# An attention stage in which half of the probabilities' turns move from TensorE to VectorE and a trip through DRAM

## The chip, the cores and the metric

The kernel runs on one core of one Trainium2 chip. The metric is device time in microseconds, from the start to the end of one execution; lower is better. The engines are named as in the profile: PE is TensorE (matmuls and transposes), DVE is VectorE, ACT is ScalarE, POOL is GpSimd, SP is SyncE, which here only issues DMAs. Profiles come from one profiled execution.

## The reference

One layer of a diffusion backbone over 1024 latent tokens and 256 context tokens, model width 1024, in float32: a SwiGLU feed-forward half step, then a short convolution branch beside an attention branch, merged by gates, then a second feed-forward half step. The part that matters here is the attention: 8 query heads and 2 key/value heads of 128, each latent query reads all 256 context keys and all 1024 latent keys in one softmax.

```python
def gqa_attend(q, k, v):
    s = jnp.einsum('btkgd,blkd->bkgtl', q, k, preferred_element_type=jnp.float32) * (HEAD_DIM ** -0.5)
    p = jax.nn.softmax(s, axis=-1).astype(v.dtype)
    return jnp.einsum('bkgtl,blkd->btkgd', p, v)
...
        k_all = jnp.concatenate([k_c, k_l], axis=1)
        v_all = jnp.concatenate([v_c, v_l], axis=1)
        o_l = latent_attention(q_l, k_all, v_all)

        x = x + ml[5] * merge_branches(y_conv_l, o_l, gt_l, w_branch_conv[layer],
                                       w_branch_attn[layer], w_out[layer])
```

## The kernel before

A product of two float32 matrices is made of three TensorE passes: each operand is split into a high part (a cast to the format float32r, on ScalarE) and a low part (the operand less its high part, on VectorE or GpSimd), and `mm3` adds high x high, high x low and low x high in one PSUM bank. `split` makes both parts.

The stages follow one another: token norms and the first feed-forward product, its output product, the mixing projections (convolution, gates, queries, keys, values), attention with the convolution branch's output product as filler, the merge of both branches, the second feed-forward step, the final norm. Nearly all tiles of 128 x 1024 float32 (4 KB a partition) come from one pool, `apool`, with 38 buffers under one tag. Weights pass through `wpool` (tags `raw`, `wh`, `wl`), short-lived 128 x 512 tiles through `tpool`. PSUM has five banks under tag `s`, two under `t` and one under `o`. The framework orders the instructions of each engine from the order of the program and a simulated timeline; where `strict` is set or an instruction is pinned, program order stays. Every engine and DMA queue works in its order.

Attention is made of 16 units (`Unit`): 8 heads by two halves of 512 queries. For a unit:
- `begin` splits the 512 queries.
- `scores(qt)`, for each of four tiles of 128 queries: TensorE makes the scores against 256 context keys and twice 512 latent keys; VectorE takes the maxima (`m3`) and the negative maximum (`nm`); ScalarE writes the exponentials to `pc` (context) and `pl` (latent, one tile of 128 x 1024 for each `qt`) with their sums (`rs`), which VectorE adds to `rsum`.
- `turn(kt)`, for each of ten key tiles (two of context, eight latent): queries stand on the partitions of `pc` and `pl`, but the product with the values needs the keys there. TensorE transposes four blocks of 128 x 128 into a PSUM bank `pt`; `split` writes the high and low parts `pts`.
- `values(kt)`: three passes with the parts of the values, added over the ten key tiles in the bank `po`.
- `inverse`: VectorE takes the reciprocals of the sums, GpSimd stores them to DRAM (`rinvd`) and loads them back as a row for all partitions (`rrow`). `output`: ScalarE copies `po` over the queries' place, GpSimd multiplies by the row.

The loop over the units runs one behind itself. While unit n makes its scores, `seconds` turns the ten key tiles of unit n - 1, three of them ahead of their `values` (`AHEAD`), and `fillers` gives single steps of the convolution branch's output product (`conv_out`, whose weights are brought in by `conv_weights` two outputs ahead). After each of the four `scores`, 3, 2, 3 and 2 steps of `seconds` are taken. The fillers are used up before the last units. After the last unit its remaining turns are mixed with `merge`, the product with the attention branch's weights. In the last units `split_output` makes the parts of finished heads on GpSimd.

Of the kernel before, what the change touches and what calls it, by code (L numbers as in the profile page):

```python
# [18 lines left out]
P = 128  # L19
D = 1024  # L20
KD = D // P
# [16 lines left out]
A_BUFS = 38  # L38
# [13 lines left out]
def tile_dit_layer(  # L52
# [52 lines left out]
    dram = ctx.enter_context(tc.tile_pool(name="dram", bufs=1, space=DRAM))  # L105

# [6 lines left out]
    def atile(name, shape=(P, SLOT), dt=F32):  # L113
        return apool.tile(list(shape), dt, tag="A", name=uniq(name))

# [333 lines left out]
    class Latents:  # L449


        def __init__(self, name):
            self.name, self.t = name, {}

        def pair(self, k, i):
            if (k, i) not in self.t:
                self.t[k, i] = atile(self.name, (P, 2, 512))
            return self.t[k, i]
# [6 lines left out]
    class Context:  # L465
        def __init__(self, name, dt=F32):
            self.t = [atile(name, (P, 4, CT), dt) for _ in range(2)]
# [49 lines left out]
    def fetch_rows(w, js):  # L517

        ts = {j: atile("raw") for j in js}
        for j, t in ts.items():  # L520
            load(t[:], w[j * P : (j + 1) * P, :])
        return ts
# [11 lines left out]
    class Winograd:  # L534
# [6 lines left out]
        def __init__(self, xs, gain, mod, m, pairs, plain=False, ahead=3, side_from=None):  # L541
# [12 lines left out]
            self.source, self.ready = self.lefts(pairs, side_from), []  # L554

        def keep(self, i, k, src, lo_eng=None):

            t = atile(f"r{i}", (P, 2, 512), F32R)
# [40 lines left out]
        def norm1(self, turned=None):  # L599
# [8 lines left out]
            def scaled(k):  # L608
                t22[k] = ttile("h22")
                if self.plain:  # L610
                    self.r[0][k] = atile("h12", (P, 2, 512))
                    t12[k] = self.r[0][k][:, 0]
# [26 lines left out]
        def part_second(self, k):  # L639

            t = self.r[0][k]
            h = atile("r0", (P, 2, 512), F32R)
            split(t[:, 0], h[:, 0], h[:, 1])
# [133 lines left out]
        def start_by_half(self):  # L777

            uc = [atile("uc", (P, 2, 512)) for _ in range(2)]
# [23 lines left out]
            for j in range(BY_HALF, self.n_ahead):  # L803
                t = atile("uc", (P, 2, 512))
# [39 lines left out]
    class Rows:  # L844


        def __init__(self, src, n, name):
# [3 lines left out]
            for k, m in self.groups:  # L851
                for lower in range(2):
                    if m == 1:
                        t = atile(name, (P, 2, 512))
# [21 lines left out]
    def row_products(w, rows, add, after=lambda i, k: None, halves=False):  # L876
# [12 lines left out]
        s1, s2, w11 = {}, {}, {}  # L889
# [13 lines left out]
        def parts(src, where):  # L903
# [3 lines left out]
            else:  # L907
                if where == "kept":
                    t = atile("kept", (P, 2, 512), F32R)
# [19 lines left out]
        def second_sum(k, m):  # L929
            s2[k] = atile("ws", (P, 2, 512))[:, :m]  # L930
# [3 lines left out]
        def sums(i, g):  # L934
# [11 lines left out]
            if i == 1 and g >= 3 or i == 4 and g < n - 3:  # L946
                k, m = groups[g - 3 if i == 1 else n - 3 + g]
                s1[k] = atile("ws", (P, 2, 512))[:, :m]
# [94 lines left out]
    xs, xc = Latents("x"), Context("xc")  # L1043

    def fetch_tokens(ch):
# [3 lines left out]
        for j in range(n // P):  # L1049
            t = atile("xtok")  # L1050
# [168 lines left out]
    def side(j, bank=ps_o):  # L1219
        pc = bank()  # L1220

        def do(i, w):
# [9 lines left out]
            if i == 4:  # L1232
                if j % 2 == 0:
                    hid_c[j // 2] = atile("hidc", (P, 4, CT), F32R)
# [45 lines left out]
    for j in range(NH):  # L1280
# [6 lines left out]
        if j == SIDE_FROM - 1:  # L1287
# [10 lines left out]
            for token in range(2):  # L1298
                c_acc.append(atile("cacc"))
# [31 lines left out]
    xs = Latents("x1")  # L1331
# [67 lines left out]
    for i in range(KD):  # L1399
        u = atile("u")  # L1400
# [47 lines left out]
    rope_t = [atile("rope", (P, KD, HD)) for _ in range(2)]  # L1448
    for i in range(2):
        sp.dma_start(out=rope_t[i][:], in_=rope[i])  # L1450
    hg = atile("hg", (P, 2, HD))
# [171 lines left out]
    class Unit:  # L1623
# [3 lines left out]
        def begin(self):  # L1627
            self.qs = [ttile("qs", dt=F32R) for _ in range(2)]
            split(q_of(self.hd, self.ch), *self.qs)
            self.pc = atile("pc", (P, 4, CT))  # L1630
            self.pl = []
            self.rsum = small("rsum", 4)

        def scores(self, qt):
# [9 lines left out]
            if self.hd == 0 and self.ch[1] == 0 and qt < 2:  # L1644
                pl = wpool.tile([P, SLOT], F32, tag="raw", name=uniq("pl"), bufs=3)
            else:
                pl = atile("pl")
            self.pl.append(pl)
            for j in range(2):
# [4 lines left out]
                parts.append((pl[:, j * 512 : (j + 1) * 512], ps))  # L1654
# [3 lines left out]
            dve.reduce_sum(out=self.rsum[:, qt : qt + 1], in_=rs[:], axis=AX.X)  # L1658

        def turn(self, kt):  # L1660
# [18 lines left out]
        def inverse(self):  # L1679
# [3 lines left out]
            pool.dma_start(out=row.rearrange("(j p) -> p j", p=P), in_=rinv[:])  # L1683
            self.rows = ttile("rrow")
            pool.dma_start(out=self.rows, in_=row.partition_broadcast(P))
# [270 lines left out]
```

## Time and profile before

| | |
|---|---|
| median of 3 runs | 2629.52 us (2629.28 to 2633.78) |
| profiled execution | 2628.72 us |
| its span, first to last instruction | 2626.9 us |
| busy: PE, DVE, ACT, POOL | 2604.6, 1988.4, 1167.3, 546.3 us |
| mean granted TensorE clock | 0.998 |
| DMA | 384.71 MB, mean 146 GB/s |

How to read it: busy time is the time in which an engine had an instruction in work; on TensorE matmuls are pipelined and their durations overlap, so a price of one is read from start to start. A row of instructions names line, engine, operation, the tile written and the tiles read, then the count; in grouped rows there follow busy time, mean duration in ns, and the idle time of the engine before them with what ended it. All instructions stand under line 90, the helper that records them, so groups are told apart by the names of tiles.

### The profile page before, as it was taken

To read this page: it belongs to the slowest core of one execution; us is meant where nothing else is said; L and a number is where in the kernel's file an instruction comes from. 1 tells how busy PE (TensorE), PEld (TensorE's weight loads), DVE (VectorE), ACT (ScalarE), POOL (GpSimd) and SP (SyncE) were. 2 spreads that over 40 slices of the span, in tenths; PEclk is the share of its full clock that TensorE was granted. 3 is DMA by queue.
4 is the path that set the end of the run, shared out by engine and by line. 5 is a ranking of instruction groups with operands and counts; after the bars stand their busy time and mean duration, and the time that the engine had idled before them with its cause. 6 is when DMAs were issued, how large, how long until landed. Compare 5 with 4: busy or idle time off the path is not lost.

```text
span 2626.9 us, 35317 instructions
## 1 busy us (share of the span) xinstructions
PE 2604.6 (99%) x12643; PEld 2173.7 (83%) x12643; DVE 1988.4 (76%) x3339; ACT 1167.3 (44%) x2322; POOL 546.3 (21%) x425
## 2 busy tenths in 40 slices
PE   8999999999999999999999999999999999999998
PEld 5888898888888888888888888888888888888888
DVE  5889866878897888977788666675457786667996
ACT  6533454333454642333345566574237223334553
POOL 0135201221010034333022112132000442321100
PEclk9999999999999999999999999999999999999999
DMA  9666475335973364532522322114525653227831
GB/s 325 205 205 200 138 216 172 119 118 201 311 185 117 127 204 158 171 126 90 200 76 92 79 87 65 33 37 121 160 81 177 196 172 97 89 84 279 197 82 65
DMA packets 377321, 384.71 MB, mean 146 GB/s; under 512 B 24102, under 2 KB 260792, under 8 KB 377144
## 3 DMA queue, kind: packets, MB, share of 16 engines
q1 hardware_dynamic: 367704, 363.53, 42.7%
q0 software_dynamic: 9440, 18.91, 4.2%
q8 instruction: 99, 1.62, 0.3%
q14 instruction: 78, 0.64, 0.1%
HBM read 310.45 MB, written 71.86 MB: 146 GB/s over the span
## 4 chain that ended last, share of the span: by engine, by line
PE 93%; DVE 3%; DMA 1%; ACT 1%; SPq 1%; issue 0%; DVEq 0%; ACTq 0%
PE ps L90 80%; PE pt L90 7%; PE po L90 6%; DMA rawm<-in_w_mod_dram 1%; SPq L90 1%; DVE xb L90 0%; DVE wl L90 0%; DVE m L90 0%; DVE macc L90 0%; ACT x L90 0%; DVE pts L90 0%; DVE nt L90 0%; ACT r L90 0%; DMA half<-in_ffn_w_in_dram 0%; DVE y L90 0%
## 5 line engine op out<-in xcount | busy, mean ns | idle before, releaser
L90 PE MATMUL ps<-r,wl 128*128 128x512 f32 x5196 | 1197.1, 390 | 2.6 <-ACT r L90 1.6
L90 PEld LDWEIGHTS ps<-r,wl 128*128 128x128 f32 x5196 | 972.5, 188 | 205.5 <-ACT r L90 1.8
L90 ACT CAST wl<-sum 128x512 fp32r<-128x512 f32 x218 | 133.8, 621 | 317.7 <-PE ps L90 240.7
L90 ACT CAST wl<-raw 128x512 fp32r<-128x512 f32 x287 | 177.7, 620 | 206.5 <-PE ps L90 155.6
L90 DVE TENSOR_TENSOR wl<-raw,wl 128x512 fp32r<-128x512 f32 x287 | 208.9, 731 | 63.3 <-ACT wl L90 61.8
L90 POOL TENSOR_TENSOR sum<-raw 128x512 f32<-128x512 f32 x55 | 79.6, 1447 | 688.0 <-DMA raw<-in_w_in_dram 221.7
L90 DVE TENSOR_TENSOR wl<-sum,wl 128x512 fp32r<-128x512 f32 x218 | 191.4, 879 | 37.6 <-ACT wl L90 36.4
L90 DVE TENSOR_TENSOR u<-u,ps 128x512 f32<-128x512 f32 x186 | 126.5, 680 | 33.1 <-PE ps L90 33.0
L90 DVE SCALAR_TENSOR_TENSOR macc<-rawm,silu_r,macc 128x512 f32<-128x512 f32 x165 | 136.7, 850 | 17.0 <-DMA rawm<-in_w_mod_dram 16.8
L90 ACT CAST rh<-hid 128x512 fp32r<-128x512 f32 x132 | 81.7, 621 | 135.5 <-PE ps L90 109.6
L90 DVE TENSOR_TENSOR pts<-pt,pts 128x512 fp32r<-128x512 f32 x160 | 107.2, 685 | 36.1 <-ACT pts L90 34.3
L90 POOL TENSOR_TENSOR sum<-raw,sum 128x512 f32<-128x512 f32 x55 | 76.7, 1394 | 273.0 <-DVE wl L90 270.0
L90 DVE TENSOR_REDUCE m<-ps 128x1 f32<-128x256 f32 (+1 forms) x192 | 110.9, 596 | 29.5 <-PE ps L90 28.4
L90 ACT CAST pts<-pt 128x512 fp32r<-128x512 f32 x160 | 92.2, 597 | 85.5 <-PE pt L90 84.6
L90 PE MATMUL ps<-rh,wl 128*128 128x512 f32 x360 | 122.1, 390 | 0.0
L90 PE MATMUL ps<-wh,r 128*128 128x512 f32 x384 | 120.4, 393 | 0.0
L90 ACT CAST wh<-raw 128x512 fp32r<-128x512 f32 (+1 forms) x85 | 68.1, 802 | 108.4 <-PE ps L90 86.2
L90 DVE TENSOR_TENSOR rl<-hid,rh 128x512 fp32r<-128x512 f32 x132 | 90.1, 686 | 27.9 <-ACT rh L90 15.8
L90 PE MATMUL ps<-kl,qs 128*128 128x512 f32 x384 | 104.0, 394 | 0.1
L90 PE MATMUL ps<-rh,wh 128*128 128x512 f32 x300 | 102.2, 389 | 0.0
L90 PE MATMUL ps<-y,wc 128*128 128x512 f32 x384 | 95.3, 391 | 0.2 <-DVE g L90 0.2
L90 POOL TENSOR_TENSOR sum<-sum,raw 128x512 f32<-128x512 f32 x55 | 88.0, 1601 | 6.0 <-PE ps L90 4.0
(333 smaller groups left out, 5064.9 us busy)
## 6 DMA issues: line engine op xcount, KB each, us to landing
raw<-in_ffn_w_in_dram SPq DMA_DIRECT2D x131, 512.0 KB
raw<-in_ffn_w_out_dram SPq DMA_DIRECT2D x72, 512.0 KB
rawm<-in_w_mod_dram SPq DMA_DIRECT2D x136, 256.0 KB
raw<-in_w_in_dram SPq DMA_DIRECT2D x64, 512.0 KB
hid<-hd SPq DMA_DIRECT2D x40, 512.0 KB
ucd<-uc SPq DMA_DIRECT2D x33, 512.0 KB
ws<-in_ffn_w_out_dram POOLq DMA_DIRECT2D x26, 512.0 KB, 6.1
hd<-c SPq DMA_DIRECT2D x42, 256.0 KB
```

The lines of the kernel that those rows point to most:

```text
L90: inst = getattr(self.engine, name)(*args, **kw)
```

## The change

For the first 256 queries of each unit the latent part of the probabilities is no longer transposed by TensorE.

- `scores(0)` and `scores(1)` write their latent exponentials into one tile `pb` (128 x 2048), with the columns of both query tiles alternating in blocks of 32. `scores(2)` and `scores(3)` write to `pl`, now one tile of 2 x 1024.
- `place`: VectorE transposes `pb` in place, in blocks of 32 x 32, in two instructions of 128 x 1024. Four DMAs on SyncE's queue store the 32-partition quarters of `pb` to a DRAM tile `turned` in runs of 64 elements; one more DMA loads it as `placed` (128 x 8 x 256) with the keys on the partitions, in runs of 256 elements. The steps of `place` are taken after the second scores of a unit (second step), after the third (first and second step) and after the fourth (first step).
- `turn(kt)` for the eight latent tiles makes two transposes instead of four, and two splits of 256 columns instead of one of 512: one from `placed`, one from `pt`. For the two context tiles four transposes stay, with the first two written in blocks, so that the columns of the first 256 queries come in the same order as in `placed`. `output` copies `po` in two parts, the first with its columns put back in order.
- The reciprocals' store goes with the values of key tile 2 and the load (`spread`) with those of key tile 4; before, both went with key tile 4.
- `apool` has 28 buffers instead of 38. A second pool takes the same room: 10 buffers of 4 KB a partition before and after attention (`btile`, tag `B`), 5 of 8 KB in attention (tag `Q`: `pb`, `pl`, `placed`). In the other stages certain tiles are taken from the second pool.

The core of the diff:

```diff
-A_BUFS = 38
+A_BUFS, B_BUFS, Q_BUFS = 28, 10, 5
...
+    def share(tag, bufs):
+
+        if shared:
+            shared.pop("guard").__exit__(None, None, None)
+        guard = tc.tile_pool(name=uniq("share"), bufs=bufs, reuse_waits="tile")
+        shared.update(guard=guard, pool=guard.__enter__(), tag=tag)
...
+    def btile(name, shape=(P, SLOT), dt=F32):
+        return shared["pool"].tile(list(shape), dt, tag=shared["tag"], name=uniq(name))
...
-            self.pc = atile("pc", (P, 4, CT))
-            self.pl = []
-            self.rsum = small("rsum", 4)
+            self.pc, self.pb, self.pl = atile("pc", (P, 4, CT)), btile("pb", (P, 2048)), btile("pl", (P, 2, SLOT))
+            self.done, self.rsum = 0, small("rsum", 4)
...
+            blocks = self.pb[:].rearrange("p (j b q c) -> p j q b c", j=2, q=2, c=32)
             for j in range(2):
...
-                parts.append((pl[:, j * 512 : (j + 1) * 512], ps))
+                if qt < 2:
+                    parts.append((blocks[:, j, qt], ps.rearrange("p (b c) -> p b c", c=32)))
+                else:
+                    parts.append((self.pl[:, qt - 2, j * 512 : (j + 1) * 512], ps))
...
+        def place(self):
+
+            for half in range(2):
+                part = self.pb[:, half * 1024 : (half + 1) * 1024]
+                dve.transpose(out=part, in_=part)
+                yield
+            turned = dram.tile([32, 32, 4, 64], F32, name=uniq("turned"))
+            for i in range(4):
+                sp.dma_start(
+                    out=turned[:, :, i].rearrange("b r f -> r b f"),
+                    in_=self.pb[i * 32 : (i + 1) * 32].rearrange("r (b f) -> r b f", b=32),
+                )
+            yield
+            self.placed = btile("placed", (P, KD, 256))
+            sp.dma_start(out=self.placed[:], in_=turned.rearrange("(k j) r i f -> (j r) k (i f)", j=4))
...
-            pt = ps_t()
-            for qt in range(4):
-                src = self.pc[:, qt, kt * P : (kt + 1) * P] if kt < 2 else self.pl[qt][:, (kt - 2) * P : (kt - 1) * P]
-                transpose(pt[:, qt * P : (qt + 1) * P], src)
             pts = wpool.tile([P, 2, 512], F32R, tag="wh", name=uniq("pts"), bufs=W_BUFS)
-            split(pt, pts[:, 0], pts[:, 1])
+            if kt < 2:
+                pt = ps_t()
+                first = pt[:, :256].rearrange("p (i q c) -> p q i c", i=4, q=2)
+                for qt in range(4):
+                    out = first[:, qt] if qt < 2 else pt[:, qt * P : (qt + 1) * P]
+                    transpose(out, self.pc[:, qt, kt * P : (kt + 1) * P])
+                split(pt, pts[:, 0], pts[:, 1])
+            else:
+                pt = ps_t(256)
+                for qt in range(2):
+                    transpose(pt[:, qt * P : (qt + 1) * P], self.pl[:, qt, (kt - 2) * P : (kt - 1) * P])
+                split(self.placed[:, kt - 2], pts[:, 0, :256], pts[:, 1, :256])
+                split(pt, pts[:, 0, 256:], pts[:, 1, 256:])
...
-            act.copy(out=of, in_=self.po)
+            v = lambda t, by: t[:, :256].rearrange(by, i=4, q=2)
+            act.copy(out=v(of, "p (q i c) -> p q i c"), in_=v(self.po, "p (i q c) -> p q i c"))
+            act.copy(out=of[:, 256:], in_=self.po[:, 256:])
...
+            if kt == 2:
+                u.inverse()
             if kt == 4:
-                u.inverse()
+                u.spread()
...
+    share("Q", Q_BUFS)
...
-            u.scores(len(u.pl))
-            for _ in range(n):
+            u.scores(u.done)
+            for i in range(n):
+                if (u.done, i) == (2, 1):
+                    place = u.place()
+                if (u.done, i) in ((2, 1), (3, 0), (3, 1), (4, 0)):
+                    run(place, 1)
                 run(rest, 1)
```

More of the change, by code (lines that the diff above doesn't have):

```diff
@@ L465, in tile_dit_layer, with __init__ @@
     class Context:
-        def __init__(self, name, dt=F32):
-            self.t = [atile(name, (P, 4, CT), dt) for _ in range(2)]
+        def __init__(self, name, dt=F32, get=btile):
+            self.t = [get(name, (P, 4, CT), dt) for _ in range(2)]
         def __call__(self, k, ch=CC):
@@ L517, in fetch_rows @@
     def fetch_rows(w, js):
-        ts = {j: atile("raw") for j in js}
+        ts = {j: btile("raw") for j in js}
         for j, t in ts.items():
@@ L641, in part_second @@
             t = self.r[0][k]
-            h = atile("r0", (P, 2, 512), F32R)
-            split(t[:, 0], h[:, 0], h[:, 1])
+            h = btile("r0", (P, 2, 512), F32R)
+            split(t, h[:, 0], h[:, 1])
             self.r[0][k] = h
@@ L777, in start_by_half @@
         def start_by_half(self):
-            uc = [atile("uc", (P, 2, 512)) for _ in range(2)]
+            uc = [btile("uc", (P, 2, 512)) for _ in range(2)]
             def second(j, t):
@@ L908, in parts @@
                 if where == "kept":
-                    t = atile("kept", (P, 2, 512), F32R)
+                    n_kept[0] += 1
+                    t = (btile if n_kept[0] <= 8 else atile)("kept", (P, 2, 512), F32R)
                 else:
@@ L929, in second_sum @@
         def second_sum(k, m):
-            s2[k] = atile("ws", (P, 2, 512))[:, :m]
+            s2[k] = (btile if halves and len(s2) < B_BUFS - 2 - len(groups) else atile)("ws", (P, 2, 512))[:, :m]
             act.activation(out=s2[k], in_=s1[k], func=AF.Copy, scale=-1.0)
@@ L947, in sums @@
                 k, m = groups[g - 3 if i == 1 else n - 3 + g]
-                s1[k] = atile("ws", (P, 2, 512))[:, :m]
+                s1[k] = (btile if halves or i == 4 and g < 2 else atile)("ws", (P, 2, 512))[:, :m]
                 load(s1[k], block(k, m, 0, 1))
@@ L1446, in v_tile @@
         return v_hi[(kt - 2) // 4][:, (kt - 2) % 4], v_lo[(kt - 2) // 4][:, (kt - 2) % 4]
-    rope_t = [atile("rope", (P, KD, HD)) for _ in range(2)]
+    rope_t = [btile("rope", (P, KD, HD)) for _ in range(2)]
     for i in range(2):
         sp.dma_start(out=rope_t[i][:], in_=rope[i])
-    hg = atile("hg", (P, 2, HD))
+    hg = btile("hg", (P, 2, HD))
     pg = ps_t(2 * P)
@@ L1683, in inverse, with spread @@
             pool.dma_start(out=row.rearrange("(j p) -> p j", p=P), in_=rinv[:])
+            self.row = row
+        def spread(self):
             self.rows = ttile("rrow")
-            pool.dma_start(out=self.rows, in_=row.partition_broadcast(P))
+            pool.dma_start(out=self.rows, in_=self.row.partition_broadcast(P))
         def output(self):
             of = q_of(self.hd, self.ch)
-            act.copy(out=of, in_=self.po)
+            v = lambda t, by: t[:, :256].rearrange(by, i=4, q=2)
+            act.copy(out=v(of, "p (q i c) -> p q i c"), in_=v(self.po, "p (i q c) -> p q i c"))
+            act.copy(out=of[:, 256:], in_=self.po[:, 256:])
             pool.tensor_mul(out=of, in0=of, in1=self.rows)
@@ L1744, in tile_dit_layer @@
         u.scores(qt)
+        if qt == 2:
+            place = u.place()
+            run(place, 2)
+        if qt == 3:
+            run(place)
         if qt < 3:
@@ L1788, in tile_dit_layer @@
     split_output(NQ - 1, C1, late=True)
+    share("B", B_BUFS)
     for j in range(KD):
@@ L1796, in tile_dit_layer @@
     fast = Winograd(xs, None, modl, 6, column_pairs(ffn2_w_in[0], ffn_offsets), ahead=AH3)
+    fast.shared_forms = [(i, k) for i in (4, 7, 6) for k in range(4)][:B_BUFS]
     first = fast.norm0()
```

47 lines of the change are left out of this document (25 added, 22 removed).

## The prediction

> **What bounds the kernel now.** I read the profile page first: the busy totals and the chain that ended last.
>
> ```profile
> span 2626.9 us, 35317 instructions
> PE 2604.6 (99%) x12643; PEld 2173.7 (83%) x12643; DVE 1988.4 (76%) x3339; ACT 1167.3 (44%) x2322; POOL 546.3 (21%) x425
> PE 93%; DVE 3%; DMA 1%; ACT 1%; SPq 1%; issue 0%; DVEq 0%; ACTq 0%
> ```
>
> TensorE (PE) works all the time and carries 93% of the chain, so time taken from TensorE can be time of the kernel, if the other engines keep up. The change acts in the attention stage alone (that the tile pools are cut up elsewhere is costed below), so the second view is the busy time by stretch there. I set the stretches by the reciprocals' stores on GpSimd (POOL), one for each unit (first and last of the sixteen shown); 1715.07 is the one after the last convolution output.
>
> ```profile
> 1453.91 0.84 POOL L90 DMA_DIRECT2D rinvd<-rinv  x1 [29.63 <-DMA g<-gcd]
> ...
> 1788.26 0.80 POOL L90 DMA_DIRECT2D rinvd<-rinv  x1
> core 0: us, PE busy (x) PEld busy (x) DVE busy (x) ACT busy (x) POOL busy (x), PEclk, DMA share, GB/s
> 1453.91:1546.22 92.31, 90.23 (x490) 74.58 (x489) 63.86 (x139) 62.05 (x154) 19.03 (x16) 1.00 0.34 92
> 1546.22:1715.07 168.85, 168.70 (x921) 141.68 (x920) 108.26 (x234) 101.57 (x258) 30.41 (x27) 1.00 0.17 46
> 1715.07:1788.26 73.19, 72.30 (x415) 60.25 (x413) 54.87 (x125) 53.92 (x143) 32.10 (x37) 1.00 0.17 48
> 1502.00:1526.00 24.00, 23.21 (x131) 19.16 (x130) 20.20 (x44) 17.80 (x47) 5.34 (x5) 1.00 0.45 143
> ```
>
> The stretches hold 4, 7 and 4 units: 23.1, 24.1 and 18.3 us a unit. In the first two TensorE also has convolution outputs as filler; in the last it has none. VectorE (DVE) works 16.0, 15.5 and 13.7 us a unit. TensorE idles 2.1, 0.2 and 0.9 us in them. So attention is bound by TensorE, with VectorE second: 69, 64 and 75%, and 84% in the 24 us in which the second half's convolution inputs are split.
>
> **The TensorE transposes that go.** Before, each key tile of a unit has four transposes; after, the eight latent tiles of each of 16 units have two. That is 2 x 8 x 16 = 256 of 640. Their price comes from start to start, because the busy times of pipelined matmuls overlap.
>
> ```profile
> 1439.99 0.38 PE L90 MATMUL pt<-ident,pc 128*128 128x128 f32 x2
> 1440.12 0.94 PE L90 MATMUL ps<-kl,qs 128*128 128x512 f32 x3
> 1440.90 0.38 PE L90 MATMUL pt<-ident,pc 128*128 128x128 f32 x2
> ...
> 1610.30 0.60 PE L90 MATMUL pt<-ident,pl 128*128 128x128 f32 x4
> 1610.65 0.48 PE L90 MATMUL po<-pts,vh 128*128 128x512 f32 x1
> 1610.96 0.40 PE L90 MATMUL po<-pts,vl 128*128 128x512 f32 x1
> 1611.20 0.39 PE L90 MATMUL po<-pts,vh 128*128 128x512 f32 x1
> 1611.43 0.60 PE L90 MATMUL pt<-ident,pl 128*128 128x128 f32 x4
> ```
>
> A product follows the one before it after 0.23 us (1611.20 to 1611.43). Four transposes and three products take 1.13 us, so the four take 0.43; two and three products take 0.91, so the two take 0.21. Each tile saves 0.22 us: 128 x 0.22 = 28.2 us, or 1.76 us a unit.
>
> **What VectorE gets.** Two in-place transposes of 128x1024 a unit, and for each of eight tiles two low parts of 256 columns where one of 512 stood. No VectorE transpose is in this trace; its bounds are the cheapest and the dearest 128x1024 operation, and halves are priced by the maxima of both widths.
>
> ```profile
> L90 DVE TENSOR_SCALAR xtok<-xtok,rs_y 128x1024 f32<-128x1024 f32 x6 | 4.2, 749 | 0.8 <-PE po L90 0.7
> L90 DVE TENSOR_TENSOR wc<-raw,wc 128x1024 fp32r<-128x1024 f32 x7 | 9.1, 1294 | 0.4 <-ACT wc L90 0.4
> L90 DVE TENSOR_REDUCE m<-ps 128x1 f32<-128x512 f32 x126 | 84.3, 684 | 13.9 <-PE ps L90 12.9
> L90 DVE TENSOR_REDUCE m<-ps 128x1 f32<-128x256 f32 x63 | 26.4, 420 | 15.6 <-PE ps L90 15.4
> ```
>
> A transpose moves one element after another like the two-operand row and has nothing that speaks for the fast single-operand one, so I take 1.2 us (0.75 to 1.3). Two halves cost 2 x 0.42 - 0.67 = 0.17 us more than a whole by busy time (0 if halves overlap fully). That is 2.4 + 1.4 = 3.8 us a unit, between 1.5 and 4.0.
>
> Unit by unit this decides what is kept:
> - Without filler (4 units): VectorE 13.7 + 3.8 = 17.5 us, TensorE 18.3 - 1.76 = 16.5. VectorE becomes the bound. With 0.4 us of its waits left a unit takes 17.9, and 0.4 of 1.76 us is kept: 5.4 us given back over four.
> - With filler, 1546 to 1715 (7 units): VectorE 19.3 of 22.4 us, 86%. At 75% TensorE idled 0.9 of 73 us (1.2%); at 86% I take 2.5%, 0.55 us a unit, 3.9 us in all.
> - The first four: 19.8 of 21.3 us, 93%, and the stretch of the convolution inputs (20.2 of 24 us) goes over 100%. I take 1.0 us a unit, 4.0 in all.
>
> **ScalarE** likewise casts halves.
>
> ```profile
> L90 ACT CAST pts<-pt 128x512 fp32r<-128x512 f32 x160 | 92.2, 597 | 85.5 <-PE pt L90 84.6
> L90 ACT ACTIVATE pl<-ps,nm 128x512 f32<-128x512 f32 x128 | 87.2, 693 | 0.0
> L90 ACT ACTIVATE pc<-ps,nm 128x256 f32<-128x256 f32 x64 | 30.8, 481 | 41.6 <-DVE nm L90 41.5
> ```
>
> A half costs some 0.39 us against 0.60 (an estimate: less the 0.21 us between the exponentials of both widths), 8 x 0.18 = 1.5 us a unit, and each output is copied in two parts, 0.2 us more. In the last stretch it works 13.5 + 1.7 = 15.2 us of 17.9: no bound, costed at nothing; without VectorE's 17.5 us as cover it would be the next at 15.2.
>
> **The way through DRAM.** Four stores of 1024 runs of 256 bytes and one load of 1024 runs of 1 KB a unit, on SyncE's queue. By isolated transfers:
>
> ```profile
> 1654.97 0.38 SPq L90 DMA_DIRECT2D raw<-in_w_branch_attn_dram  x1
> 1655.50:1658.00 2.50, 2.50 (x15) 2.06 (x14) 1.70 (x5) 1.68 (x4) 0.68 (x1) 1.00 0.71 215
> 1668.51 0.32 SPq L90 DMA_DIRECT2D zd<-g  x1
> 1668.50:1670.50 2.00, 2.00 (x11) 1.65 (x10) 1.51 (x4) 1.38 (x3) 0.79 (x1) 1.00 0.35 131
> 1670.50:1671.00 0.50, 1.00 0.37 4
> 1669.22 0.79 POOL L90 DMA_DIRECT2D rinvd<-rinv  x1 [13.04 <-DVE rinv L90]
> 1678.05 0.56 POOL L90 DMA_DIRECT2D rrow<-rinvd  x1 [8.04 <-DMA rinvd<-rinv]
> ```
>
> The last columns are the busy share of 16 DMA engines and GB/s. A weight load of 1024 runs of 512 bytes takes 0.71 x 2.5 us x 16 / 1024 = 28 ns a run; a store of 128 runs of 2 KB takes 0.35 x 2.0 x 16 / 128 = 88 ns. On the line through both a run of 256 bytes takes 18 ns and one of 1 KB 48 ns. Each engine has 256 small runs (4.6 us) and 64 large ones (3.1 us); with 1 us around each, the weight load's 3.0 us from issue to end less its 1.8, the placed block is there 9.7 us after the second VectorE transpose. Busy share: 7.7 us of a unit on top of 17%, so the engines have room. When must it be there? The transpose is issued about at key tile 5, the first placed tile is read at tile 2 of the next unit.
>
> ```profile
> 1725.16 0.60 PE L90 MATMUL pt<-ident,pl 128*128 128x128 f32 x4
> ...
> 1736.93 0.27 PE L90 MATMUL pt<-ident,pl 128*128 128x128 f32 x1
> ...
> 1611.43 0.60 PE L90 MATMUL pt<-ident,pl 128*128 128x128 f32 x4
> ...
> 1628.74 0.60 PE L90 MATMUL pt<-ident,pl 128*128 128x128 f32 x4
> ```
>
> There are 11.8 us without filler and 17.3 with it. Tight in the first, and VectorE runs late there: I put 0.2 us on each of four units and 1.5 us on the last one, whose tiles follow with little between: 2.3 us. The load waits on SyncE's queue for the stores, about 6 us; behind it stand weight loads and gates of convolution outputs that come a unit or more ahead (one weight load and one gate a unit), so I cost that at nothing; without that lead the first late thing would be a convolution's weights.
>
> **Reciprocals.** The store now goes at key tile 2 and the load at tile 4. GpSimd's queue then does not stand still for the 8.0 us shown above; behind it are weight subtractions, the products with the rows and, at the end, the splits of outputs. No wait of TensorE hangs on them, and the rows are needed at tile 9: nothing, either way. The pools: 38 buffers become 28 and 10 (five double ones in attention), the same memory; a buffer that comes free in the wrong pool can hold up a load in any stage. I take 0, within plus or minus 4 us.
>
> Sum: -28.2 + 5.4 + 3.9 + 4.0 + 2.3 = -12.6 us. The profiled execution took 2628.72 us, 0.8 under the median of 2629.52; 2629.5 - 12.6 = 2617.
>
> **Rivals.**
> - A, all of it is kept: the VectorE transposes cost 0.75 us, halves overlap, and VectorE's 13.7 + 1.5 = 15.2 us stay under TensorE's 16.5. Then 2629.5 - 28.2 = 2601. For it speaks the single-operand row, against it the two-operand one; chance 0.14.
> - B, VectorE's waits stay. In the last stretch it idled 18.3 us, 4.6 a unit, behind scores, exponentials and casts. If half of it stays when it is the bound, a unit without filler takes 17.5 + 2.3 = 19.8 us, 1.5 more than now: +6; the seven keep 1.0 each, -7; the first four keep nothing; with the 2.3 us of the DRAM way, +1: 2630, no change. Chance 0.16.
> - C, slower: the small stores end late. The 2 KB of reciprocals moved by 1671.0 (0.37 of the engines, 4 GB/s), and yet their reader was released at 1678.05: 32 writes of 4 bytes an engine took 7 us more, some 0.2 us each. If runs of 256 bytes pay anything like this, ScalarE stands before the first placed tile and the scores' banks fill behind it. At 36 ns a run the block is there after 14.3 us, 2.5 late in five units: 12.5 us, and the gain is gone; that is the point from which it decides. At 45 ns it is 4.8 late in five: 24 us, 2641. At 0.2 us a run, 51 us a unit, hundreds of us. For it speaks that row; against it, that those runs are 64 times smaller and share their lines. Chance 0.20, a third of it above 2641.
>
> [...]
>
> **How the numbers follow.** A measurement here tells 0.2%, 5.3 us. The forecast has 0.50, A 0.14, B 0.16, C 0.20. Faster: the forecast and A, 0.64. Same: B, less a little that goes over, and C near its turning point, 0.17. Slower: most of C and the edge of B, 0.19. The forecast's own range is 2607 to 2624 (VectorE's added 4.0 or 2.5 us, pools plus or minus 4). The range from A to C at 45 ns, 2601 to 2641, leaves out C's far end and a little below A.
>
> **What would show it.** After, 384 transposes on `pt` in attention instead of 640; 32 VectorE transposes of 1.2 us; VectorE over 90% busy in units without filler, and TensorE waiting there on VectorE. A unit without filler near 17.9 us and one with filler near 22.9. If ScalarE's casts wait for the DMA of `placed`, C is at work; if the attention stage gains 13 us and the kernel does not, the pools are. The forecast is wrong if VectorE's transpose is far from 1.2 us, if a run of 256 bytes takes over 36 ns, or if TensorE waits at other stages' buffers.

## The result, and the profile after

The changed kernel takes 2698.97 us (median; 2685.1 to 2706.03) against 2631.13 us before: a ratio of 1.0251, 95% interval 1.0207 to 1.0294. The forecast was 2617; by the medians it got 68 us slower. The profiled execution took 2685.1 us, the fastest of the four, so the views below account for some 56 us.

The busy totals and the chain of the page after:

```profile
span 2683.3 us, 35285 instructions
PE 2608.9 (97%) x12387; PEld 2153.1 (80%) x12387; DVE 2053.3 (77%) x3499; ACT 1181.5 (44%) x2466; POOL 549.1 (20%) x425
PE 86%; DVE 5%; DMA 4%; issue 2%; ACT 2%; SPq 1%; POOL 0%; DVEq 0%; ACTq 0%; POOLq 0%
```

The 256 matmuls are gone (12643 to 12387), but TensorE's busy time rose by 4 us, and its share of the chain fell from 93 to 86%. The windows below cover the same units as in the prediction (first four, seven with filler, last four); here they begin at the reciprocals themselves, 0.6 us ahead of the stores:

```profile
core 0: us, PE busy (x) PEld busy (x) DVE busy (x) ACT busy (x) POOL busy (x), PEclk, DMA share, GB/s
1461.58:1561.89 100.31, 90.57 (x444) 71.98 (x443) 81.73 (x181) 65.86 (x192) 18.91 (x15) 0.97 0.63 162
1561.89:1736.25 174.36, 161.41 (x791) 127.81 (x790) 130.93 (x302) 108.67 (x320) 30.44 (x26) 0.98 0.48 128
1736.25:1839.88 103.63, 75.26 (x358) 58.33 (x357) 79.41 (x167) 58.25 (x180) 34.94 (x39) 0.87 0.48 116
```

Before, these stretches took 92.3, 168.9 and 73.2 us, and TensorE idled 2.1, 0.2 and 0.9 us in them. Now it idles 9.7, 13.0 and 28.4, and its busy time in the three together is only 4 us less (327.2 against 331.2): part of the work runs at a lower clock (0.97, 0.98 and 0.87). Outside attention the kernel is later too: the last store of `yd`, ahead of attention, starts at 1254.1 us instead of 1246.5, and from the merge's last matmuls (2027.5 instead of 1976.1) to the last `kept` product (2671.3 instead of 2614.9) it loses another 5.0. Such a delay of the same event against the kernel before is called lag here. So about 8 us are lost ahead of attention, 44 in it and the merge, 5 after.

What TensorE and ScalarE waited for in attention (in all, times, longest, us), and the low parts of the placed blocks on VectorE (ns, min/median/max):

```profile
PE pt L90 <- DVE pts L90: 26.6, 23, 8.0
PE ps L90 <- ACT pts L90: 10.2, 1, 10.2
PE ps L90 <- ACT pc L90: 6.0, 6, 2.7
...
ACT pts L90 <- DMA placed<-turned: 20.9, 6, 11.3
...
L90 DVE TENSOR_TENSOR pts<-placed,pts x128: 381/419/8911, 1468.0 to 1857.0; 128x256 fp32r<-128x256 f32 x128
```

Before, TensorE waited 1.7 us in all for VectorE's `pts`. Two new waits stand out: VectorE's low parts, of up to 8.91 us where the median is 0.42, and ScalarE in front of the placed block. The timeline of VectorE, then GpSimd, then TensorE around the longest one:

```profile
1823.61 1.24 DVE L90 STREAM_TRANSPOSE pb<-pb 128x1024 f32<-128x1024 f32 x1
1824.76 0.39 DVE L90 TENSOR_TENSOR pts<-pt,pts 128x256 fp32r<-128x256 f32 x1
1825.07 8.91 DVE L90 TENSOR_TENSOR pts<-placed,pts 128x256 fp32r<-128x256 f32 x1
1833.90 0.41 DVE L90 TENSOR_TENSOR pts<-pt,pts 128x256 fp32r<-128x256 f32 x1
...
1824.08 1.27 POOL L90 TENSOR_TENSOR q<-q,rrow 128x512 f32<-128x512 f32 x1
1825.31 1.28 POOL L90 TENSOR_TENSOR ol<-q,oh 128x512 fp32r<-128x512 f32 x1
...
1831.22 2.47 POOL L90 TENSOR_TENSOR ol<-q,oh 128x512 fp32r<-128x512 f32 x2
...
1834.37 0.69 PE L90 MATMUL pt<-ident,pl 128*128 128x128 f32 x2 [7.97 <-DVE pts L90]
```

Three operations of VectorE run while GpSimd works. The transpose (one operand in SBUF) and the low part with `pt` in PSUM take their usual time (1.24 and 0.39 us). The low part of `placed`, with both operands in SBUF, does not end until GpSimd's unbroken row of operations has ended at 1833.69 (1831.22 + 2.47): the product under way and nine more, of which the first and the last row are shown. The rest of the trace says the same: 14 of the 128 low parts of `placed` took more than 0.6 us (0.91 to 8.91), and each of them ran while an operation of GpSimd did; of the other 114 one did. Of the 160 low parts of `pt` 27 ran beside GpSimd, and none was held up (0.69 us at most, for 512 columns).

The clock after two such stops:

```profile
1744.00:1748.00 4.00, 0.00 (x0) 0.00 (x0) 0.00 (x0) 0.00 (x0) 0.58 (x1) 0.57 0.53 86
1748.00:1756.00 8.00, 3.18 (x9) 2.46 (x10) 2.72 (x5) 3.64 (x12) 0.00 (x0) 0.50 0.33 88
1832.00:1840.00 8.00, 5.63 (x19) 4.58 (x20) 6.22 (x15) 4.38 (x14) 1.70 (x2) 0.50 0.75 241
```

TensorE's clock is at 0.50 when it starts again (at 1752.82 and at 1834.37), so these two stops (gaps in its work) are paid beyond their length: a product follows the one before it after 0.42 us (1835.29 to 1835.71), where it took 0.24 ahead of the stop (1825.78 to 1826.02). In windows of 1 us the clock is 0.78 in 1744 to 1745 and 0.90 in 1758 to 1759, 0.50 between these two; it is 0.94 in 1829 to 1830 and in 1840 to 1841, and 0.50 between these two. By that it fell some 2.0 and 3.5 us after TensorE's last work (1742.57 and 1826.41) and was back at 1758.2 and 1840.1, after 5.4 and 5.7 us at half clock from the restart.

### The profile page after: what moved, and what is told of

It reads as the page before. It is cut to its first block, busy times and chain, and to the rows that moved or that the text cites. A ratio compares the mean times of both kernels' runs of the same rounds, so it can differ in the third digit from the quotient of the medians.

```text
span 2683.3 us, 35285 instructions
## 1 busy us (share of the span) xinstructions
PE 2608.9 (97%) x12387; PEld 2153.1 (80%) x12387; DVE 2053.3 (77%) x3499; ACT 1181.5 (44%) x2466; POOL 549.1 (20%) x425
## 4 chain that ended last, share of the span: by engine, by line
PE 86%; DVE 5%; DMA 4%; issue 2%; ACT 2%; SPq 1%; POOL 0%; DVEq 0%; ACTq 0%; POOLq 0%
PE ps L90 75%; PE pt L90 5%; PE po L90 5%; DVE pts L90 2%; DMA rawm<-in_w_mod_dram 1%; SPq L90 1%; DVE m L90 1%; DVE pb L90 1%; DMA placed<-turned 1%; DMA turned<-pb 1%; ACT pts L90 0%; DMA g<-gcd 0%; DMA rinvd<-rinv 0%; DVE macc L90 0%; DVE wl L90 0%
## 5 line engine op out<-in xcount | busy, mean ns | idle before, releaser
L90 DVE SCALAR_TENSOR_TENSOR macc<-rawm,silu_r,macc 128x512 f32<-128x512 f32 x165 | 135.2, 840 | 21.7 <-DMA rawm<-in_w_mod_dram 21.6
L90 DVE TENSOR_REDUCE m<-ps 128x1 f32<-128x512 f32 (+1 forms) x192 | 111.5, 594 | 29.4 <-PE ps L90 27.8
L90 ACT CAST pts<-pt 128x256 fp32r<-128x256 f32 (+1 forms) x160 | 67.1, 428 | 74.2 <-PE pt L90 73.5
L90 DVE TENSOR_TENSOR pts<-placed,pts 128x256 fp32r<-128x256 f32 x128 | 79.4, 628 | 16.6 <-ACT pts L90 16.3
L90 POOL TENSOR_TENSOR sum<-sum,raw 128x512 f32<-128x512 f32 x55 | 88.3, 1606 | 10.2 <-DMA ucd<-uc 3.8
```

The lines of the kernel that those rows point to most:

```text
L90: inst = getattr(self.engine, name)(*args, **kw)
```

## The experiments

Three causes were suspected: the pools (a buffer free in the wrong pool; theory S in the expectations), the trip through DRAM (late blocks; T), and VectorE's low parts held up by GpSimd (L). The rival to all three is that VectorE is simply full (V). Ratios are to the kernel before on the same chip; its medians differ by up to 1.8 us between the chips, so differences between runs of different chips are good to that. The code cuts are shortened, with `...` or with lines joined.

**One cause at a time, in the changed kernel.** The pools alone: cut as after, with the attention code of before (the second pool stays at 10 buffers of 4 KB; the five double ones are not in this run).

```diff
-A_BUFS = 38
+A_BUFS, B_BUFS, Q_BUFS = 28, 10, 5
...
-                pl = atile("pl")
+                pl = btile("pl")
```

> Only the pools are cut in two (28 and 10 buffers, the same tiles in the second pool in every other stage); attention is that of the kernel before, with its latent tiles from the second pool. Theory S (the pools cost time outside attention: the same events stand 8 us later before attention and another 7 us later after it): 8 to 18 us slower than before, with the lag at the start of the queries' splits near 8 us. Theories L, T and V (all in attention): within 4 us of before.

2649.73 us, 1.0070 (1.0053 to 1.0087): 18.8 us for the pools alone. By the profiled run's lag 4.9 us are lost ahead of attention, 11.7 in it and 5.3 after. Inside, one stop stands out, in the stretch where the second half's convolution inputs are fetched; ScalarE had waited 6.2 us for the load of one of them:

```profile
PE po L90 <- ACT pts L90: 5.2, 2, 5.1
```

The trip left out: `placed` is `pb`, read where it lies.

```diff
-            for i in range(4): sp.dma_start(out=turned[:, :, i]..., in_=self.pb[i * 32 : ...])
-            sp.dma_start(out=self.placed[:], in_=turned...)
+            self.placed = self.pb[:].rearrange("p (k n) -> p k n", k=KD)
```

> The five DMAs of a unit are left out; the placed tile is the turned one itself, so the probabilities of the first 256 queries stand in the wrong order. Theory T (the placed block lands late: ScalarE waited 20.9 us for it, TensorE 10 us behind that, and its clock fell to 0.5 after the stop): 20 to 35 us faster than the changed kernel, no wait of ScalarE on a DMA. Theory L (VectorE's low parts of the placed tile stand while GpSimd works, up to 8.9 us): at most 12 us faster, operations of over 1 us on the low parts remain. Theory V (VectorE is simply full): at most 5 us faster.

2666.84 us, 1.0139 (1.0123 to 1.0154): 32 us under the changed kernel. That is in T's range and above L's limit of 12, yet the long low parts stay (up to 7.74 us, 32.2 us of TensorE's waits).

The low part of a placed block takes its first operand from PSUM instead of `placed`.

```diff
-                split(self.placed[:, kt - 2], pts[:, 0, :256], pts[:, 1, :256])
+                act.copy(out=pts[:, 0, :256], in_=self.placed[:, kt - 2])
+                dve.tensor_sub(out=pts[:, 1, :256], in0=pt, in1=pts[:, 0, :256].bitcast(F32))
```

> The low part of the placed half takes its first operand from PSUM (the bank of the other half) instead of from the placed tile: the same engine, width and count, one operand in SBUF instead of two; the low part's values are wrong. Theory L: no low part above 0.7 us (628 ns mean becomes about 420), 20 to 35 us faster than the changed kernel. Theory T: at most 10 us faster. Theory V: same, as VectorE's work is the same.

2677.32 us, 1.0178 (1.0163 to 1.0193): 21.7 us under the changed kernel, in L's range and above T's limit of 10. No low part of 256 columns took over 0.43 us. So both causes are at work, and what they cost overlaps.

The reciprocals' store and load both at key tile 4, as before.

```diff
-            if kt == 2:
-                u.inverse()
             if kt == 4:
+                u.inverse()
                 u.spread()
```

> The changed kernel with both of the reciprocals' DMAs back at key tile 4. If that part of the change matters neither way, within 6 us of the changed kernel (2685 to 2706). If the earlier store is what puts GpSimd's work in VectorE's way, 10 us or more faster.

2693.42 us, 1.0239 (1.0211 to 1.0266), inside the interval of the changed kernel: this edit does nothing that shows.

**The whole change with one pool.** One pool of 38 buffers as before; `pb`, `pl` and `placed` in tiles of 4 KB, and the trip in two halves, so that the first starts after the first VectorE transpose (the cut is against the changed kernel).

```diff
-self.pb, self.pl = btile("pb", (P, 2048)), btile("pl", (P, 2, SLOT))
+self.pb, self.pl = [atile("pb") for _ in range(2)], {}
...
+            dve.transpose(out=self.pb[0][:], in_=self.pb[0][:]); store(0)
+            yield
+            dve.transpose(out=self.pb[1][:], in_=self.pb[1][:]); store(1)
+            yield; fetch(0); yield; fetch(1)
```

> The whole change, but all tiles from one pool of 38 buffers: the turned, the kept and the placed tiles are cut into tiles of 4 KB a partition, and the trip through DRAM is made in two halves (store after each VectorE transpose, two loads), so the first half of the keys need not wait for the second. Theory S: 12 to 18 us faster than the changed kernel from the other stages alone, and none of the 8 us lag before attention. Theory T adds 10 to 25 us. Theory L alone: the long low parts remain, and it stays slower than the kernel before by 15 to 30 us.

2661.79 us, 1.0117 (1.0102 to 1.0132): 37 us under the changed kernel. The lag ahead of attention is gone (1247.5), and ScalarE waits 1.9 us for placed blocks instead of 20.9. What is left lies in VectorE (its low parts, and what TensorE waited for) and in one wait on SyncE's queue:

```profile
L90 DVE TENSOR_TENSOR pts<-placed,pts x128: 378/412/6084, 1460.0 to 1839.6; 128x256 fp32r<-128x256 f32 x128
PE pt L90 <- DVE pts L90: 30.1, 25, 6.5
...
ACT y L90 <- DMA y<-yd: 4.6, 1, 4.6
```

Three ways round the long low parts followed, all with one pool: on GpSimd, from PSUM, and with GpSimd's weight parts and head splits moved to VectorE and ScalarE. The first of them also moves the reciprocals' load to key tile 7.

```diff
# on GpSimd
+split(self.placed[...], pts[:, 0, :256], pts[:, 1, :256], pool)
-if kt == 4: u.spread()
+if kt == 7: u.spread()
# from PSUM
+dve.tensor_sub(out=pts[:, 1, :256], in0=pt, in1=pts[:, 0, :256].bitcast(F32))
# GpSimd quiet
-conv_weights(j + 2, pool); split_output(next(to_split), C0, C1)
+conv_weights(j + 2); split_output(next(to_split), C0, C1, late=True)
```

> One pool and half tiles as before in this study; the low parts of the placed tiles on GpSimd, and the load of the reciprocals at key tile 7, so that GpSimd's queue does not stand in front of the low parts. Theory L (VectorE's operations with two SBUF operands stand behind GpSimd's): no VectorE operation on `pts` above 0.8 us, TensorE's idle time in attention falls from 43 to under 20 us, 2600 to 2620 us. Theory V (VectorE is full in units without filler): it loses 3.4 us of work a unit and is at 14.2 us against TensorE's 16.5, so V expects the same gain in the last units only, 2635 to 2650. Rival: GpSimd's low parts come late and TensorE waits for them: above 2650.

> One pool and half tiles, and VectorE's low parts of the placed half with their first operand from PSUM (wrong values of the low part); VectorE's work is the same in count and width. Theory L: with the pools, the trip and the standing VectorE all gone, 2605 to 2625 us. Theory V: what is left is VectorE's added 3.8 us a unit, and it stays at 2630 to 2650 us, with VectorE over 95% busy in the units without filler.

> One pool and half tiles; GpSimd's tensor work that can go elsewhere is moved: the low parts of the convolution weights to VectorE, the splits of the finished heads to ScalarE and VectorE; GpSimd keeps the products with the reciprocals' rows (1.3 us, one a unit). Theory L: no low part above 1.8 us (6.1 us was the longest with them), 10 to 25 us faster than with GpSimd's work in place, in spite of some 21 us more on VectorE. Theory V: 5 to 20 us slower, since VectorE gets that work.

2662.44 (1.0118, 1.0100 to 1.0136), 2665.88 (1.0137, 1.0121 to 1.0153) and 2660.38 us (1.0118, 1.0102 to 1.0134): none moved the time, and what L had named was missed three times (2600 to 2620, 2605 to 2625, 10 to 25 us faster). Each shows other waits in the old one's place. In the first TensorE waits 23.9 us for GpSimd's `pts`. In the second it waits 17.2 us for ScalarE's casts and 16.5 us for VectorE's `pts`, though none of these is long any more; the low part of a placed block now depends on `pt` too, and VectorE stood 17.5 us for it. In the third it waits 12.4 and 7.4 us for ScalarE's `pc` and `pts`, and 19.5 us for VectorE's `pts` remain, with VectorE's added work. So these three take the long low parts away, or nearly (1.95 us at most in the third), and cannot say what they cost.

**What is left with one pool: by leaving work out.** First the trip; then GpSimd's arithmetic of the attention stage too; then VectorE's transposes too; and GpSimd's arithmetic left out of the kernel before, as the counterpart.

```diff
# no trip
+            self.placed = [t[:].rearrange("p (k n) -> p k n", k=4) for t in self.pb]
# GpSimd's arithmetic
-        split(raw[:], hi[:], lo[:], lo_eng)
+        act.copy(out=hi[:], in_=raw[:])        # low part = high part
-            pool.tensor_mul(out=of, in0=of, in1=self.rows)
-                pool.tensor_copy(out=hi, in_=q_of(hd, ch)); pool.tensor_sub(...)
+                act.copy(out=hi, in_=q_of(hd, ch))
# VectorE's transposes
-            dve.transpose(out=self.pb[0][:], in_=self.pb[0][:])
```

> The whole change with one pool (2661.8 us), but the blocks that VectorE turned are read where they lie: no stores to DRAM, no load, and so the 128-row blocks stand in another order (that part of the result is left out). Trip theory (with one pool the trip still delays key tiles and stands ahead of the convolution inputs on SyncE's queue): about 2648, what the run without the trip (2666.8) had above the run of the pools alone (18.8 dearer than before). No-trip-cost theory: 2660 or more; the waits for VectorE's low parts (30 us) carry the loss alone. Both expect TensorE's waits for the low parts to stay near 30 us.

> The run before this one, and GpSimd's arithmetic of the attention stage left out: the low parts of the convolution weights and of the head outputs and the products with the reciprocals' rows are not computed (high parts stand in their place), so that nothing of GpSimd can hold VectorE up. Lock theory (VectorE's two-operand operations stand while GpSimd works, and this carries what is left): no low part over 0.7 us, and the kernel comes under its counterpart without GpSimd's arithmetic and without the change, by 8 to 28 us: about 2605 to 2620. Work theory (VectorE's added 3.8 us a unit alone makes it the bound, lock or not): within 5 us of that counterpart or over it, 2630 to 2645, with VectorE over 85% busy.

> The run before this one, also without VectorE's 32 transposes (the blocks are read as they are; their order within is left out of the result). 32 x 1.24 = 40 us less on VectorE. Work theory: 15 to 40 us faster than the run before this one. Lock theory: up to 8 us faster, since with nothing to stand for VectorE has room; the 28 us of TensorE's transposes were then already kept in the run before this one.

> The kernel before with GpSimd's arithmetic of the attention stage left out in the same way: the counterpart of the two runs before. TensorE was 99% busy in attention, so 2624 to 2631 on either theory; 2615 or less would say that GpSimd's operations held up the kernel before as well.

Without the trip 2663.8 us (1.0118, 1.0103 to 1.0133): no better than with it. Without GpSimd's arithmetic 2631.84 (0.9994, 0.9985 to 1.0004): 32 us better, though 2605 to 2620 had been expected if the long low parts were all that was left. Without the 32 transposes 2621.55 (0.9956, 0.9941 to 0.9971): 10.3 more, between what the two theories had named, so VectorE's added work costs something as well. The counterpart is slower than before, 2643.92 (1.0044, 1.0027 to 1.0061), against both expectations: one stop of 6.1 us behind ScalarE, whose cast of a weight waited 6.9 us for its load. The run without GpSimd's arithmetic is 12.1 us under this counterpart, part of which is that stop. The low parts and TensorE's wait for them, without the trip and then also without GpSimd's arithmetic:

```profile
L90 DVE TENSOR_TENSOR pts<-pb,pts x128: 381/418/5497, 1460.3 to 1839.2; 128x256 fp32r<-128x256 f32 x128
PE pt L90 <- DVE pts L90: 31.6, 27, 5.9
```

```profile
L90 DVE TENSOR_TENSOR pts<-pb,pts x128: 382/418/430, 1461.9 to 1805.9; 128x256 fp32r<-128x256 f32 x128
PE pt L90 <- DVE pts L90: 9.5, 15, 1.5
```

The same instruction goes from 5497 to 430 ns at most, with the same median. A late result of GpSimd is not what went: in the run that keeps its arithmetic no wait of TensorE, VectorE or ScalarE between 1440 and 1830 us is put down to GpSimd.

**GpSimd's reads, or its work as such?** The suspicion is that VectorE stands only against operations of GpSimd that read; the expectations call it the port theory, by the author's guess at the reason, which no run shows. GpSimd's subtractions, casts and products become fills of the same tiles: it writes, and reads nothing. Beside it the same in the kernel before, and the trip put back in the run without GpSimd's arithmetic.

```diff
-            pool.tensor_mul(out=of, in0=of, in1=self.rows)
+            pool.memset(of, 0.5)
-                pool.tensor_copy(out=hi, in_=q_of(hd, ch)); pool.tensor_sub(...)
+                pool.memset(hi.bitcast(F32), 0.5); pool.memset(lo.bitcast(F32), 0.0)
```

> The run with one pool and without the trip (2663.8 us), but each of GpSimd's sums, casts and products of the attention stage is put in as a fill with a constant of the same tile: GpSimd writes as before and reads nothing (low parts of weights, head outputs and the products with the reciprocals are left out of the result). Port theory (VectorE stands only against operations of GpSimd that read): low parts of at most 0.7 us and a time near the run without GpSimd's arithmetic, 2628 to 2636. Any-GpSimd-work theory: low parts of several us stay, 2645 to 2664.

> The whole change with one pool, trip and all, and GpSimd's arithmetic of the attention stage left out (as in the run that gave 2631.8 us without the trip). If the trip is hidden once pools are out of the way: within 5 us of that run, 2627 to 2637. If it was covered until now by the waits for the low parts: 2642 or more, with ScalarE waiting for the placed blocks or for the convolution inputs behind them on SyncE's queue.

> The kernel before, with the same fills in the place of GpSimd's sums, casts and products: the counterpart of the run with fills. TensorE was 99% busy, so 2626 to 2633 on either theory; and 12 us more, as in the counterpart with the operations left out, only if a stop at a convolution weight's or input's load comes with it.

With fills 2627.62 us (0.9983, 0.9974 to 0.9992), its counterpart 2638.3 (1.0026, 1.0014 to 1.0037; again a stop behind ScalarE, 4.6 us). The fills, the low parts beside them, and the three stretches of the run with fills:

```profile
L90 POOL MEMSET wc<- 128x1024 f32 x9 | 8.7, 963 | 19.4 <-PE ps L90 19.4
L90 POOL MEMSET q<- 128x512 f32 x16 | 8.6, 540 | 46.5 <-ACT q L90 46.5
L90 POOL MEMSET oh<- 128x512 f32 x14 | 7.6, 544 | 0.0
L90 POOL MEMSET ol<- 128x512 f32 x14 | 7.6, 543 | 0.0
...
L90 DVE TENSOR_TENSOR pts<-pb,pts x128: 381/414/427, 1461.7 to 1802.5; 128x256 fp32r<-128x256 f32 x128
...
1455.90:1549.10 93.20, 88.60 (x450) 71.19 (x449) 76.33 (x182) 67.96 (x195) 11.29 (x16) 1.00 0.32 80
1549.10:1709.61 160.51, 155.59 (x788) 125.00 (x786) 123.92 (x302) 106.19 (x317) 16.98 (x25) 1.00 0.21 48
1709.61:1785.48 75.87, 69.56 (x358) 53.28 (x355) 65.24 (x166) 58.56 (x180) 20.72 (x40) 1.00 0.19 43
```

53 fills are there, and no low part takes over 0.43 us, the 13 that ran beside a fill included: here VectorE's low part with two SBUF operands stood behind operations of GpSimd that read (up to 8.91 us in the changed kernel), not behind those that only write. A fill is shorter (0.54 us against 1.3 for the product), but up to eight follow one another without a gap, and nothing stood behind such a row either. So GpSimd's writes are ruled out as the cause, and its reads are left. By what means they hold VectorE up was not shown; in the timeline above it waited 8.91 us, through ten instructions of GpSimd in a row, not through one.

With the trip put back and GpSimd's arithmetic left out 2639.15 us (1.0028, 1.0017 to 1.0040), 7.3 over the run without it, a little outside what was expected if it were hidden. ScalarE's splits of the convolution inputs, whose loads are on the same queue, then stand behind it:

```profile
ACT y L90 <- DMA placed<-turned: 5.7, 1, 5.7
```

**Does it pay in part?** The change in the seven units with filler only, one pool, trip and all, with everything computed; then the weights' low parts there on VectorE; then the products there too, from PSUM.

```diff
+            self.blocks = 4 <= 2 * hd + (ch == C1) <= 10
...
-                conv_weights(j + 2, pool)
+                conv_weights(j + 2)
...
-            act.copy(...); act.copy(...); pool.tensor_mul(out=of, in0=of, in1=self.rows)
+            dve.tensor_mul(out=..., in0=self.po..., in1=self.rows...)
```

> One pool, and the blocks are turned on VectorE and placed through DRAM in seven units only (the fifth to the eleventh, those with filler); the other nine units are as before. If the change pays where VectorE has room: TensorE's 7 x 1.76 = 12.3 us are saved and some 4 to 8 given back, 2623 to 2628. By the stretches measured (167.8 us with the change and one pool against 168.9 before) it saves one us: 2628 to 2632, not to be told from before. Slower than 2636 only if passing from one kind of unit to the other stops TensorE.

> The run of seven units (2634.9 us), with the low parts of the second half's convolution weights on VectorE (one of about 1.2 us a unit) instead of GpSimd (2.4 us). Port theory: GpSimd then holds VectorE for one product of 1.3 us at a time, so no low part of a placed block over 1.8 us; of the 8 us that the seven units gained in the run with fills, half goes to VectorE's weights: about 2627. If VectorE's added work is what counts: 2633 or more.

> The run before this one, and in those seven units the product with the reciprocals' row is made by VectorE from PSUM (0.42 + 2 x 0.42 us at most, with ScalarE's copies gone), so that GpSimd reads nothing there. Port theory: no low part over 0.7 us, 2624 to 2628. If VectorE's work is what counts (about 2 us more a unit than in the seven-unit run, some 21 of 22.4 us): 2631 or more.

2634.91 us (1.0012, 1.0003 to 1.0022), 2634.57 (1.0009, 1.0000 to 1.0018) and 2630.6 (0.9995, 0.9986 to 1.0004). The longest low part of a placed block falls from 4.00 to 1.82 to 0.68 us, as the port theory says, but the times that it named (about 2627, then 2624 to 2628) were missed. That VectorE's added work and the trip take the rest is likely, and not shown. The last cannot be told from the kernel before; no complete kernel here beats it. In the first of the three the hold-up shows in its plainest form (VectorE, then GpSimd):

```profile
1631.49 4.00 DVE L90 TENSOR_TENSOR pts<-placed,pts 128x256 fp32r<-128x256 f32 x1 [0.30 <-ACT pts L90]
...
1631.54 1.31 POOL L90 TENSOR_TENSOR q<-q,rrow 128x512 f32<-128x512 f32 x1
1632.79 2.40 POOL L90 TENSOR_TENSOR wc<-raw,wc 128x1024 fp32r<-128x1024 f32 x1
```

The low part ends at 1635.49, the weight's at 1635.19. By the record it had begun 0.05 us before the product, and was held up all the same.

## Why the prediction was wrong

**The main step that failed: the low parts' price.** The prediction priced "two halves" at 0.17 us more than a whole, by VectorE's maxima of both widths (`m<-ps`), whose one operand lies in PSUM, and took the duration as a property of the shape. `placed` lies in SBUF, and so do both operands of its low part. The median held (0.42 us), but the mean came to 628 ns against 416 for `pts<-pt,pts`: 128 x 0.21 = 27 us of VectorE, in 14 operations of 0.91 to 8.91 us. TensorE stopped for 8.0 us behind the longest, with half clock after it. Taking GpSimd's reads away gave 36.2 us (2663.8 to 2627.6) with fills and 32.0 by leaving the work out. No rival had this mechanism: B put VectorE's waits down to dependences, and came to 2630.

The profile before held the sign. Two rows of one shape, the first from outside attention with both operands in SBUF, the second with one in PSUM (busy us, mean ns):

```profile
L90 DVE TENSOR_TENSOR wl<-sum,wl 128x512 fp32r<-128x512 f32 x218 | 191.4, 879 | 37.6 <-ACT wl L90 36.4
L90 DVE TENSOR_TENSOR pts<-pt,pts 128x512 fp32r<-128x512 f32 x160 | 107.2, 685 | 36.1 <-ACT pts L90 34.3
```

In the trace 65 of the first took over 0.8 us (up to 1.79), and all 65 ran beside an operation of GpSimd; 40 of the second did, and none took over 0.70 us.

**The trip, 2.3 us in the sum.** In the changed kernel leaving it out gave 32 us. With one pool and halves it cost nothing beside the long low parts, and 7.3 us once those were gone. The sign of rival C was seen (20.9 us of ScalarE's waits for the placed block), but not its mechanism. In the trace's DMA records of the changed kernel, within attention, a run of 256 bytes took 18 ns (median of 65536) and one of 1 KB 46 ns, against 18 and 48 in the forecast; no small store was dear. The stores and the load took a median of 4.6 and 5.6 us from issue to landing, together near the 9.7 forecast. What failed is that every trip was taken as undisturbed. By the same records 15 of the 16 loads had moved their last run within 4.6 to 7.0 us of their issue; one, issued at 1737.91 just after the stores had moved their last run (1737.38), took 14.1 us. ScalarE was released at 1752.36, and TensorE's stop of 10.2 us is the wait for it. What held that load up stays open, and so does whether the pools, the whole tiles or the load's wait on all four stores made the difference between 32 and 0. "Costed at nothing" for what stands behind the load was wrong too: not weights but the convolution inputs were late (5.7 us).

**The pools, 0 within plus or minus 4.** Alone they cost 18.8 us, 10.2 of it outside attention, where the changed kernel loses 12.6 (7.6 and 5.0). The prediction itself named the sign ("if the attention stage gains 13 us and the kernel does not, the pools are"), but its bounds came from no row. Which buffers came free too late was not traced.

The causes do not add: the trip is worth 32 us in the changed kernel, nothing beside the long low parts with one pool, and 7.3 us without them. The likely reason is that a TensorE that stands for one of them does not wait for the next. From the changed kernel down, one pool with halves gave 37 us and the fills in place of GpSimd's reads 36 (with the trip left out, which gave nothing by itself there); what is left, 2627.6, is 4.3 under the kernel before.

**What held.** 256 transposes went, and VectorE's transpose takes 1.24 us (1.2 taken; that it moves one element after another was the author's guess, the trace shows the time alone); without all 32 the time fell by 10.3 us. The reciprocals' move cost nothing that shows. With the fills, in the run that has no reads of GpSimd, no trip and no split pools, the unit sums can be read: the seven units with filler take 160.51 / 7 = 22.9 us, as forecast; the last four 75.87 / 4 = 19.0, between the forecast's 17.9 and B's 19.8; the first four 93.2 us, 0.9 more than before where 3.0 less was forecast. So of the 28.2 us 8.3 are kept with filler, and 3.6 are lost again in the other units: 4.8 in these stretches, and 4.3 by the medians against the kernel before. Against the counterpart with the same fills it is 10.7 us, but that one has the stop of 4.6 us named above. The way of the sum was right; its part for units without room was too kind, and without its trip it had forecast 14.9 us, ahead of the costs above.

**VectorE over 90% busy in the last units** was not seen: 79.4 of 103.6 us (77%) in the changed kernel, and with the fills 65.24 of 75.87 us (86%), with TensorE at 92%. Neither is full; that the unit is set there by the chain from scores to exponentials to casts to products is likely, and was not tested.

## What to carry to other kernels

Price an added operation by a row whose operands lie in the same memories, not only by one of the same shape, and list what GpSimd reads at that time. When a kernel's bound engine is 99% busy, look at what a new dependence does when it is late once: here late blocks and held-up low parts, with TensorE's stops of up to 10 us and the half clock after the longest, outweighed 256 saved transposes. And cut a tile pool in an experiment of its own before putting it at zero.

## What the runs showed of the hardware

A VectorE subtraction of 128 x 256 with both operands in SBUF took 8.91 us while GpSimd worked through ten reading operations without a gap, and at most 0.43 us beside fills; with one operand in PSUM the same shape took at most 0.43 us, beside GpSimd too. Two stops of TensorE, of 8.0 and 10.2 us, cost more than their length: the granted clock was 0.50 for the first 5.7 and 5.4 us of the work that followed. In the kernel before, where TensorE waited 1.7 us in all for VectorE's `pts`, with GpSimd's arithmetic left out one stop of 6.1 us went with 11 us of time (the mean clock from 1460 to 1560 us was 0.97), and with fills one of 4.6 us with 6.
